# Second score products of two 64-wide attentions: 128 rows in place of 64, and one low-key tile per head in the neighbourhood attention

## The chip, the core and the metric

The kernel runs on one core of a Trainium2 chip. The core has TensorE (PE), VectorE (DVE), ScalarE (ACT), GpSimd (POOL) and SyncE (SP), which here issues every DMA of the stages in question. The metric is the device time of one execution in microseconds. Three timed runs of the kernel before took 1984.27, 1992.58 and 1996.03 us; the median is 1992.58 us.

## The reference, cut to what matters

A two-layer backbone over 1024 latent tokens and 256 context tokens, feature width 1024. Layer 0 joins a differential attention of 4 heads with a latent attention of 8 heads; layer 1 joins an mLSTM with a neighbourhood attention of 8 heads. Two of these attentions have query and key vectors of 64 values: the differential one (two score maps per head) and the neighbourhood one. Cut to the scores:

```python
DA_HEADS, DA_QK = 4, 64
NA_HEADS, NA_DH = 8, 64
...
q1, q2, k1, k2 = (to_heads(t, DA_HEADS) for t in (q1, q2, k1, k2))
...
s_nb = jnp.einsum('bqhd,brqjhd->bhqrj', q_r, k_nb).astype(F32) * NA_SCALE + bias
s_cx = jnp.einsum('bqhd,bthd->bhqt', q_r, k_ctx).astype(F32) * NA_SCALE
p = jax.nn.softmax(jnp.concatenate([s_nb.reshape(b, h, GRID_W, n_nb), s_cx], axis=-1), axis=-1)
```

Each differential head takes softmax(q1 k1) minus a factor times softmax(q2 k2). In the neighbourhood attention each query sees a window of 8 x 16 grid cells and all 256 context tokens.

## The kernel before

Products of high accuracy are made of two parts: a value is split into a high part, which PE takes as it is, and a low part, the rest. A score is q_high k_high + q_low k_high + q_high k_low; the product of the two low parts is left out.

For 64-wide heads the kernel uses the 128 rows of PE like this. The query tile holds the high part of q in one half of its 128 partitions and the low part in the other. The high key tile kh holds the same 64 rows twice, in both halves. One product of 128 rows then gives (q_high + q_low) k_high. A second product adds q_high k_low; it uses 64 rows, namely the half in which q_high stands, and the low key tile kl.

**Attention stage of layer 0** (class `Differential`, and `Latent` for the other heads). For each differential head and each of its two score maps b, `load_scores` (L536) fills one tile `o` of 128 x 4 x 1280: slot 0 is q, slot 1 kh, slot 2 kl. It issues five DMAs of 320 KB: q and kh for each half (L543, L544), and kl for partitions 0 to 63 (L545). `load_values` (L547) loads the values and the gate. There is one tile `o` per map, so the next head's load of a map waits until the last score product of the head before has read it. For each row tile of 128 queries, `cut` (L562) issues the score products in pieces of at most 512 keys: L568 with kh (128 rows), L569 with kl (64 rows). Latent row tiles have products of 96 rows (L720 to L722). Scores go to one of two PSUM tiles `s`; DVE finds the row maximum (L1151), ACT the exponentials (L1158), DVE combines the two maps (L588); PE transposes the result into one of two banks `tp` (L1175), ACT and DVE copy it out (L518), and PE forms the value products (L599, L745).

**Neighbourhood stage of layer 1** (class `Neighbours`). Each of the 8 heads h has 8 steps (hf, g). `load` (L2094) gets q, kh, kl, the gate and, for even heads, the values in 16 pieces. Two units may be loaded at a time. kl is one shared tile for all heads: an even head uses partitions 0 to 63, an odd head 64 to 127, and each fills only its own half (L2111, one DMA of 320 KB). For odd heads the halves of q are swapped, so that q_high is in the half of kl. A step's `scores` (L2137) issues four products: L2143 (kh, 384 neighbourhood keys, 128 rows), L2144 (kl, 64 rows), L2145 (kh, 256 context keys, 128 rows), L2146 (kl, 64 rows). DVE adds the bias and finds the maximum (L2151), ACT takes exponentials (L2157), POOL scales (L2164). After two steps PE transposes the pair (L2191), copies follow (L518), then the value products (L2205). Between the steps stand filler products: gate products (L2030 to L2032), and at the end the first half of the output projection (L2289 to L2291).

In both stages the order of the instructions comes from a planner, `Plan` (L428): a task names its engine, a cost, the tasks it follows and the buffers it takes and gives back. The planner issues the task that can start earliest by its own account. Each engine then runs its instructions in that order, SP its DMA issues too.

Of the kernel before, what the change touches and what calls it, by code (L numbers as in the profile page):

```python
# [137 lines left out]
def hybrid_kernel(ctx, tc, t, out, dbg=None):  # L138
# [111 lines left out]
    def ada_first(f, w, pool, psum):  # L250
        """The layer's shift and scale of one block of 128 features."""
        ps = psum.tile([P, 512], F32, name="mm")
        for k in range(KT):
            g = 32 * (k % 4)
            T.matmul(ps[g:g + 32, :256], sil[:, k, :], w[:, k, :], start=k < 4, stop=k >= 4)
        part = pool.tile([P, 256], F32, name="part0", bufs=2)
        V.tensor_copy(out=part, in_=ps[:, :256])
        ps = psum.tile([P, 512], F32, name="mm")
        for i in range(2):
            T.matmul(ps[:, 2 * i:2 * i + 2], part[:, i * P:(i + 1) * P], cst[:, C_SEL:C_SEL + 2], start=True, stop=True)  # L260
            b = V0["ab0"] + 8 * i + f
            V.tensor_scalar(out=mods[0][:, 8 * i + f, :], in0=ps[:, 2 * i:2 * i + 2], scalar1=vt[0][:, b:b + 1],
                            scalar2=float(i), op0=ALU.add, op1=ALU.add)
# [130 lines left out]
    # ---------------------------------------------------------------- layer 0: projections  # L394
# [27 lines left out]
    class Join:  # L422
        """A buffer that several tasks give back together."""
# [4 lines left out]
    class Plan:  # L428
        """Orders the instructions of a pipelined phase: every task names its engine, about how long it holds it, what
        it follows and which buffers it takes or gives back; the earliest possible task is issued next. Kinds of  # L430
        tasks can lean: count as that much later (or earlier) than they could start."""
# [79 lines left out]
    def moves(plan, bank, dst, m, last, cut=3):  # L511
        """Copies m blocks of 128 columns out of a bank, in parts that the engines take as they come."""
        parts = [(0, m)] if m < cut else [(0, m // 2), (m // 2, m)]
        join = Join("tp", len(parts))
        left = list(parts)

        def move(eng, c0, c1):
            copy_by(eng)(out=dst()[:, c0:c1, :], in_=bank()[:, c0 * P:c1 * P].rearrange("p (c q) -> p c q", q=P))  # L518
            left.pop()
            if not left:  # L520
                given("tp", bank())
        return [plan.add("AV", (on_scalar((c1 - c0) * P, False), on_vector((c1 - c0) * P)), partial(move, c0=c0, c1=c1),
                         [last], [], [join], rank=R2) for c0, c1 in parts]
# [7 lines left out]
    class Differential(Unit):  # L531
# [4 lines left out]
        def load_scores(self, pool, b):  # L536
            h = self.h
            r = slice(64 * (h % 2), 64 * (h % 2) + 64)
            o = pool.tile([P, 4, NT], FR, name=f"o{b}")
            self.q[b], self.kh[b], self.kl[b] = o[:, 0, :], o[:, 1, :], o[0:64, 2, :]  # L540
            for i in range(2):
                hb = slice(64 * i, 64 * i + 64)
                dma(out=self.q[b][hb, :].bitcast(F32), in_=s_qk[b][i][h // 2, r, :])  # L543
                dma(out=self.kh[b][hb, :].bitcast(F32), in_=s_qk[2 + b][0][h // 2, r, :])  # L544
            dma(out=self.kl[b].bitcast(F32), in_=s_qk[2 + b][1][h // 2, r, :])  # L545
# [11 lines left out]
        def plan(self, tt):  # L557
# [4 lines left out]
            def cut(b, n0, nn):  # L562
                def emit(_):
                    if n0 == 0:
                        x["s", b] = taken("s")
                    s, ql = x["s", b], self.q[b][:, tt * P:(tt + 1) * P]
                    ks = slice(k0 * P + n0, k0 * P + n0 + nn)
                    T.matmul(s[:, n0:n0 + nn], ql, self.kh[b][:, ks], start=True, stop=False)  # L568
                    T.matmul(s[:, n0:n0 + nn], ql[0:64], self.kl[b][:, ks], start=False, stop=True)  # L569
                return emit  # L570
# [61 lines left out]
        def finish(self, t0, n, last):  # L632
            """A group of row tiles: the root mean square of every row, the gain and the gate."""
# [189 lines left out]
    with space(name="pa", bufs=1) as pa, space(name="psa", bufs=1, space=PSUM) as psa0, ExitStack() as wa_stack:  # L823
# [8 lines left out]
        def load_x(g, q):  # L832
            """A quarter of the features of a group of row tiles."""
            t0, n = TG[g]
            src = t["x"][0] if t0 < LT else t["ctx"][0]
            r0 = t0 % LT * P
            x = xp.tile([P, 4, 256], F32, name="xt", bufs=8)[:, 0:n]
            dma(out=x, in_=src[r0:r0 + n * P, q * 256:(q + 1) * 256].rearrange("(a p) n -> p a n", p=P))
            xs[g, q] = x
# [8 lines left out]
        def first_products(g, k):  # L848
            """Adds feature block k to the first weights' products of a group of row tiles, two tiles to a bank."""
# [288 lines left out]
    # ---------------------------------------------------------------- layer 0: attention  # L1138
# [154 lines left out]
    # ---------------------------------------------------------------- output projection and layer norm  # L1293
# [103 lines left out]
    # ---------------------------------------------------------------- layer 1: mLSTM  # L1397
# [337 lines left out]
    # ---------------------------------------------------------------- layer 1: projections and mLSTM  # L1735
# [107 lines left out]
    with space(name="hidc", bufs=1, side="right") as hq, space(name="zt", bufs=2, side="right") as zt, \  # L1843
# [84 lines left out]
        def chunk():  # L1928
            """The weights loaded ahead, and the load of those after the next."""
# [52 lines left out]
    # ---------------------------------------------------------------- layer 1: neighbourhood attention  # L1982
# [3 lines left out]
    with space(name="nf", bufs=1, side="right") as nf, space(name="psf", bufs=1, space=PSUM) as psf:  # L1986
# [101 lines left out]
        class Neighbours:  # L2088
# [5 lines left out]
            def load(self):  # L2094
# [3 lines left out]
                if "kl" not in sh:  # L2098
                    sh["kl"] = nf.tile([P, NT], FR, name="kl")
# [4 lines left out]
                self.kl, self.gate, self.bias = sh["kl"], sh["gate"], sh["bias"]  # L2104
# [6 lines left out]
                dma(out=self.kl[r, :].bitcast(F32), in_=s_kn[1][p, r, :])  # L2111
# [8 lines left out]
                self.v, self.x = sh["v"]  # L2120

# [6 lines left out]
            def plan(self, plan, hf, g):  # L2128
# [8 lines left out]
                def scores(_):  # L2137
# [6 lines left out]
                    T.matmul(s[:, 128:512], q[ws], kl[ws], start=False, stop=True)  # L2144
                    T.matmul(s[:, 512:768], q, self.kh[:, NLAT:NT], start=True, stop=False)  # L2145
                    T.matmul(s[:, 512:768], q[ws], self.kl[ws, NLAT:NT], start=False, stop=True)  # L2146
# [19 lines left out]
                if hf == 0 and g == 0:  # L2166
                    self.ready = plan.add("D", 14.0 if self.h % 2 == 0 else 5.0, lambda _: self.load(),
                                          stores if self.h >= 4 else [], ["unit"])
                if g == 0:
# [3 lines left out]
                self.first = last = plan.add("P", 0.54, scores, [self.ready], ["s"])  # L2173
# [53 lines left out]
        plan = Plan("neighbours", s=2, tp=2, mm=2, np=4, npt=2, eo=2, e=2, hv=2, raw=1, wr=1, unit=2, bt0=1, bt1=1, slot=0, y=2, nyy=1)  # L2227
# [8 lines left out]
        def settle_half(_):  # L2236
            """The second half of the layer's hidden rows is used up: half of the output projection's weights goes there."""
# [35 lines left out]
        def first_half(tt, opened, ready):  # L2273
            """A row tile's residual with the half of the output projection's sum that the mLSTM's features give."""
# [84 lines left out]
```

## Time and profile before

| what | value |
|---|---|
| timed runs | 1984.27, 1992.58, 1996.03 us |
| span of the profiled execution | 1998.1 us |
| span against the median | 5.5 us more |
| PE busy | 1923.2 us (96%) |
| DVE busy | 1078.6 us (54%) |
| ACT busy | 785.6 us (39%) |
| mean granted clock of PE | 0.975 |
| differential score products | from 462.4 to 975.1 us of the span |
| neighbourhood score products | from 1636.6 to 1887.7 us of the span |

The profile comes from one execution. Its own time is known as the span alone, from the first to the last instruction; it stands 2.1 us above the slowest timed run. In the rows of a timeline the columns are the start, the time, the engine, the line, the operation, what it writes and reads, rows * columns of PE in use, and the tile that it reads; behind them, in brackets, idle time before it and what ended that. Matmuls are pipelined and their ends are modelled, so two starts in a row tell more than one duration. In the rows of a window stand the length of the stretch, the busy time of PE, PE's weight load, DVE, ACT and POOL, then PE's granted clock (1.00 is full), the busy share of the DMA engines and what they moved in GB/s.

### The profile page before, as it was taken

How to read it: one execution, taken by the hardware profiler on the slowest of the kernel's cores; microseconds unless marked ns; L12 is line 12 of the kernel's file. 1: busy time of each engine (PE TensorE's matmuls, PEld its weight loads, DVE VectorE, ACT ScalarE, POOL GpSimd, SP SyncE). 2: the span in 40 equal slices, each digit the busy share in tenths (PEclk: the TensorE clock that was granted, in tenths of full speed). 3: DMA queues.
4: the chain of work that ended last, by engine and by line, in shares of the span. 5: the costliest groups of instructions: out<-in, count | busy, mean ns of one | idle time of the engine just before them, and what ended most of it. 6: DMA issues, size and time to landing. Idle time of an engine off the chain costs nothing.

```text
span 1998.1 us, 33063 instructions
## 1 busy us (share of the span) xinstructions
PE 1923.2 (96%) x12493; PEld 1590.8 (80%) x12493; DVE 1078.6 (54%) x2267; ACT 785.6 (39%) x1627; POOL 530.3 (27%) x651
## 2 busy tenths in 40 slices
PE   7999999999999999999999989999998999999998
PEld 5888998886777777778787879888898877777676
DVE  3653124313666666656665854765766125566756
ACT  2311024423556555555662312334543233344521
POOL 1433233100132222323363432220111002223434
PEclk9999999997899999999999999999999999999999
DMA  9757425675130550540566442226452365466552
GB/s 282 230 198 227 139 68 155 196 197 132 30 88 6 125 130 9 127 122 12 139 191 229 138 143 74 82 76 184 146 142 66 116 209 137 130 172 172 157 164 84
DMA packets 241475, 270.93 MB, mean 136 GB/s; under 512 B 24914, under 2 KB 203038, under 8 KB 241318
## 3 DMA queue, kind: packets, MB, share of 16 engines
q1 hardware_dynamic: 241318, 268.83, 46.9%
q8 instruction: 99, 1.62, 0.4%
q14 instruction: 58, 0.48, 0.1%
HBM read 187.90 MB, written 87.16 MB: 138 GB/s over the span
## 4 chain that ended last, share of the span: by engine, by line
PE 69%; DMA 8%; DVE 3%; SPq 1%; issue 1%; ACT 1%; POOL 0%; DVEq 0%; POOLq 0%; ACTq 0%
PE mm L390 7%; PE mm L392 7%; PE mm L391 7%; PE tp L1175 5%; PE s L569 4%; PE tp L745 3%; PE tp L599 3%; PE s L568 3%; PE mm L1778 3%; PE mm L1779 3%; PE mm L1780 3%; PE mm L2030 2%; PE tp L2205 2%; PE tp L2191 2%; DMA o<-s_qk 2%; PE s L720 2%
## 5 line engine op out<-in xcount | busy, mean ns | idle before, releaser
L1151 DVE TENSOR_REDUCE nm<-s 128x1 f32<-128x1280 f32 (+1 forms) x160 | 203.9, 1276 | 139.8 <-PE s L569 117.4
L1158 ACT ACTIVATE p<-s,nm 128x1280 f32<-128x1280 f32 (+1 forms) x160 | 185.4, 1159 | 68.1 <-DVE nm L1151 42.0
L737 POOL TENSOR_SCALAR p<-p,zs 128x512 f32<-128x512 f32 (+1 forms) x208 | 128.3, 633 | 309.9 <-DVE zs L733 282.6
L518 ACT COPY pt<-tp 128x256 f32<-128x256 f32 x346 | 119.3, 375 | 153.8 <-PE tp L1175 145.8
L1175 PE MATMUL tp<-cst,p 128*128 128x128 f32 x1008 | 162.1, 285 | 4.7 <-DVE pt L518 2.2
L347 POOL TENSOR_TENSOR wlo<-raw,whi 128x1024 fp32r<-128x1024 f32 (+2 forms) x41 | 98.9, 2413 | 214.8 <-ACT whi L339 210.3
L1175 PEld LDWEIGHTS tp<-cst,p 128*128 128x128 f32 x1008 | 117.1, 144 | 42.4 <-issue 19.6
L390 PE MATMUL mm<-whi,hhi 128*128 128x256 f32 (+1 forms) x496 | 147.6, 298 | 0.3 <-DVE z L975 0.3
L392 PE MATMUL mm<-whi,hlo 128*128 128x256 f32 (+1 forms) x496 | 146.6, 296 | 0.2 <-DVE hlo L290 0.2
L391 PE MATMUL mm<-wlo,hhi 128*128 128x256 f32 (+1 forms) x496 | 146.4, 295 | 0.0
L339 ACT CAST whi<-raw 128x1024 fp32r<-128x1024 f32 (+2 forms) x54 | 55.9, 1035 | 172.0 <-DMA raw<-in_ev_w_in_dram 71.6
L2164 POOL TENSOR_SCALAR np<-np,nrz 128x640 f32<-128x640 f32 x64 | 53.5, 838 | 241.3 <-DVE nrz L2161 236.8
L518 DVE COPY pt<-tp 128x256 f32<-128x256 f32 x158 | 64.3, 422 | 76.9 <-ACT pt L518 61.5
L569 PE MATMUL s<-o 64*128 64x512 f32 (+1 forms) x208 | 99.6, 479 | 3.3 <-DMA o<-s_qk 3.3
L568 PE MATMUL s<-o 128*128 128x512 f32 (+1 forms) x208 | 96.7, 465 | 5.7 <-DMA o<-s_qk 4.0
L390 PEld LDWEIGHTS mm<-whi,hhi 128*128 128x128 f32 x496 | 94.6, 191 | 2.6 <-issue 1.7
L392 PEld LDWEIGHTS mm<-whi,hlo 128*128 128x128 f32 x496 | 94.5, 191 | 0.5 <-DVE hlo L290 0.4
L391 PEld LDWEIGHTS mm<-wlo,hhi 128*128 128x128 f32 x496 | 94.6, 191 | 0.2
L720 PE MATMUL s<-o 96*128 96x512 f32 (+1 forms) x208 | 89.0, 428 | 0.6 <-ACT p L1158 0.6
L599 PE MATMUL tp<-v,pt 128*128 128x128 f32 x672 | 85.7, 283 | 0.0
L745 PE MATMUL tp<-pt,v 128*64 128x128 f32 x1344 | 84.3, 280 | 0.4 <-ACT pt L518 0.2
L599 PEld LDWEIGHTS tp<-v,pt 128*128 128x128 f32 x672 | 81.2, 198 | 3.1 <-DVE pt L518 0.8
(451 smaller groups left out, 5052.8 us busy)
## 6 DMA issues: line engine op xcount, KB each, us to landing
adaw<-in_ada_w_dram SPq DMA_DIRECT2D x16, 1024.0 KB
raw<-in_od_w_in_dram SPq DMA_DIRECT2D x32, 512.0 KB
o<-s_qk SPq DMA_DIRECT2D x40, 320.0 KB
raw<-in_ev_w_in_dram SPq DMA_DIRECT2D x18, 512.0 KB
bt<-s_bt SPq DMA_DIRECT2D x16, 576.0 KB
adaw<-in_ada_w_dram SPq DMA_DIRECT2D x16, 512.0 KB
o<-s_mq SPq DMA_DIRECT2D x16, 480.0 KB
s_gate<-e SPq DMA_DIRECT2D x24, 256.0 KB
```

The lines of the kernel that those rows point to most:

```text
L390: T.matmul(ps, ahi(k), bhi(k), start=k == k0, stop=False)
L391: T.matmul(ps, ahi(k), blo(k), start=False, stop=False)
L392: T.matmul(ps, alo(k), bhi(k), start=False, stop=k == nk - 1)
L518: copy_by(eng)(out=dst()[:, c0:c1, :], in_=bank()[:, c0 * P:c1 * P].rearrange("p (c q) -> p c q", q=P))
L568: T.matmul(s[:, n0:n0 + nn], ql, self.kh[b][:, ks], start=True, stop=False)
L569: T.matmul(s[:, n0:n0 + nn], ql[0:64], self.kl[b][:, ks], start=False, stop=True)
L599: T.matmul(o[:, :P], x["pt"][:, c, :], self.v[:, k0 + c, :], start=c == 0, stop=c == nch - 1)
L720: T.matmul(s[:, n0:n0 + nn], self.qh[a][:, qsl], self.kh[a][:, ks], start=True, stop=False)
L745: T.matmul(o[64 * b:64 * b + 64, :P], self.v[:, k0 + c, b * 64:(b + 1) * 64], pair[b]["pt"][:, c, :], start=c == 0, stop=c == nch - 1)
L1151: V.tensor_reduce(out=nm, in_=s[:, :w], axis=AX.X, op=ALU.max, negate=True)
L1158: S.activation(out=p[:, :w], in_=s[:, :w], func=AF.Exp, bias=nm, accum_out=z)
L1175: T.transpose(ps[:, c * P:(c + 1) * P], p()[:, (c0 + c) * P:(c0 + c + 1) * P], ident)
```

## The change

Both second products use all 128 rows. kl is now held in both halves, so the product is (q_high + q_low) k_low; the term q_low k_low, which was left out, is in it.

In the attention stage slot 2 of the tile `o` has all 128 partitions, and L545 stands inside the loop over the halves: six DMAs of 320 KB for each map, not five. Tile sizes and the planner's costs stay the same there.

In the neighbourhood stage the shared kl goes. `load_low` fills one kl tile (one buffer) for each head with two DMAs of 320 KB. It is a task of its own that follows the head's `load` and takes the buffer `kl`; the last step of a head gives it back, and the first products of a head wait for it. The cost of a step's scores in the plan goes from 0.54 to 0.58. The score products stand in L2147 to L2150 now, the transpositions in L2197, the value products in L2211, the fillers of the output projection in L2295 to L2297.

```diff
-            self.q[b], self.kh[b], self.kl[b] = o[:, 0, :], o[:, 1, :], o[0:64, 2, :]
+            self.q[b], self.kh[b], self.kl[b] = o[:, 0, :], o[:, 1, :], o[:, 2, :]
             for i in range(2):
                 hb = slice(64 * i, 64 * i + 64)
                 dma(out=self.q[b][hb, :].bitcast(F32), in_=s_qk[b][i][h // 2, r, :])
                 dma(out=self.kh[b][hb, :].bitcast(F32), in_=s_qk[2 + b][0][h // 2, r, :])
-            dma(out=self.kl[b].bitcast(F32), in_=s_qk[2 + b][1][h // 2, r, :])
+                dma(out=self.kl[b][hb, :].bitcast(F32), in_=s_qk[2 + b][1][h // 2, r, :])
...
-                    T.matmul(s[:, n0:n0 + nn], ql[0:64], self.kl[b][:, ks], start=False, stop=True)
+                    T.matmul(s[:, n0:n0 + nn], ql, self.kl[b][:, ks], start=False, stop=True)
...
-                dma(out=self.kl[r, :].bitcast(F32), in_=s_kn[1][p, r, :])
...
+            def load_low(self):
+                p, a = self.h // 2, self.h % 2
+                self.kl = nf.tile([P, NT], FR, name="kl", bufs=1)
+                for i in range(2):
+                    dma(out=self.kl[64 * i:64 * i + 64, :].bitcast(F32), in_=s_kn[1][p, 64 * a:64 * a + 64, :])
...
-                    T.matmul(s[:, 128:512], q[ws], kl[ws], start=False, stop=True)
+                    T.matmul(s[:, 128:512], q, kl, start=False, stop=True)
...
-                    T.matmul(s[:, 512:768], q[ws], self.kl[ws, NLAT:NT], start=False, stop=True)
+                    T.matmul(s[:, 512:768], q, self.kl[:, NLAT:NT], start=False, stop=True)
...
+                    self.ready_low = plan.add("D", 4.0, lambda _: self.load_low(), [self.ready], ["kl"], rank=0)
...
-                self.first = last = plan.add("P", 0.54, scores, [self.ready], ["s"])
+                self.first = last = plan.add("P", 0.58, scores, [self.ready, self.ready_low], ["s"],
+                                             ["kl"] if hf and g == 3 else [])
...
-        plan = Plan("neighbours", s=2, tp=2, mm=2, np=4, npt=2, eo=2, e=2, hv=2, raw=1, wr=1, unit=2, bt0=1, bt1=1, slot=0, y=2, nyy=1)
+        plan = Plan("neighbours", s=2, tp=2, mm=2, np=4, npt=2, eo=2, e=2, hv=2, raw=1, wr=1, unit=2, kl=1, bt0=1, bt1=1, slot=0, y=2, nyy=1)
```

In the attention stage the order on PE, DVE, ACT and POOL stays as it was. In the neighbourhood stage the planner gives another order. Two places of it follow; names carry the buffers' numbers.

PE at the change from head 6 to head 7, before: the first two steps of head 7 (L2143 to L2146) with what stands ahead of and between them; `tp` are transposition banks, `np` probabilities, `npt` their transposes, `vn` and `vx` values.

```order
L2191 MATMUL tp_15064<-cst,np_15067 128x128 x4
L2205 MATMUL tp_15063<-npt_15072,vn 64x128 x6
L2205 MATMUL tp_15063<-npt_15072,vx 64x128 x4
L2191 MATMUL tp_15064<-cst,np_15067 128x128
L2191 MATMUL tp_15064<-cst,np_15068 128x128 x3
L2143 MATMUL s_15061<-kh,q 128x384
L2144 MATMUL s_15061<-kl,q 128x384
L2145 MATMUL s_15061<-kh,q 128x256
L2146 MATMUL s_15061<-kl,q 128x256
L2191 MATMUL tp_15063<-cst,np_15068 128x128 x2
L2143 MATMUL s_15062<-kh,q 128x384
```

The same place on PE in the changed program (L2147 to L2150 are the scores, L2197 the transpositions, L2211 the value products):

```order
L2197 MATMUL tp_15072<-cst,np_15075 128x128
L2197 MATMUL tp_15072<-cst,np_15076 128x128 x3
L2197 MATMUL tp_15071<-cst,np_15076 128x128 x2
L2211 MATMUL tp_15072<-npt_15079,vn 64x128 x6
L2211 MATMUL tp_15072<-npt_15079,vx 64x128 x4
L2147 MATMUL s_15069<-kh,q 128x384
L2148 MATMUL s_15069<-kl,q 128x384
L2149 MATMUL s_15069<-kh,q 128x256
L2150 MATMUL s_15069<-kl,q 128x256
L2147 MATMUL s_15070<-kh,q 128x384
```

The first scores of head 7 moved behind all transpositions and the value products of head 6's last pair.

SP at the same head change, before: the loads of a head (q, kh, kl and the gate `ngt`), a bias table `bt` and stores of results.

```order
L2109 DMA q<-s_qn_11132 64x1024
L2110 DMA kh<-s_kn_11133 64x1280
L2109 DMA q<-s_qn_11131 64x1024
L2110 DMA kh<-s_kn_11133 64x1280
L2111 DMA kl<-s_kn_11134 64x1280
L2112 DMA ngt<-s_gate 64x1024
L2123 DMA bt_15095<-s_bt 128x3x384
L2219 DMA s_y<-nyy 64x512
```

And in the changed program:

```order
L2108 DMA q<-s_qn_11140 64x1024
L2109 DMA kh<-s_kn_11141 64x1280
L2108 DMA q<-s_qn_11139 64x1024
L2109 DMA kh<-s_kn_11141 64x1280
L2110 DMA ngt<-s_gate 64x1024
L2127 DMA bt_15102<-s_bt 128x3x384
L2124 DMA kl<-s_kn_11142 64x1280 x2
L2225 DMA s_y<-nyy 64x512
```

The low keys moved from the middle of the head's load to a place of their own behind the bias table, and there are two transfers where there was one.

More of the change, by code (lines that the diff above doesn't have):

```diff
@@ L2097, in load @@
                 sh = self.shared
-                if "kl" not in sh:
-                    sh["kl"] = nf.tile([P, NT], FR, name="kl")
+                if "gate" not in sh:
                     sh["gate"] = nf.tile([P, NLAT], F32, name="ngt")
@@ L2103, in load @@
                         G.memset(y[:, :, 384:640], 0.0)
-                self.kl, self.gate, self.bias = sh["kl"], sh["gate"], sh["bias"]
+                self.gate, self.bias = sh["gate"], sh["bias"]
                 self.q = nf.tile([P, NLAT], FR, name="q", bufs=2)
```

## The prediction

> **What bounds the kernel now.** I began with the head of the page and its chain that ended last, to see which engine carries the end, and then cut out the two stages that the change touches.
>
> ```profile
> span 1998.1 us, 33063 instructions
> PE 69%; DMA 8%; DVE 3%; SPq 1%; issue 1%; ACT 1%; POOL 0%; DVEq 0%; POOLq 0%; ACTq 0%
> ...
> 460.00:980.00 520.00, 507.46 (x3448) 387.40 (x3447) 324.79 (x588) 294.69 (x696) 128.39 (x219) 0.95 0.33 78
> 1636.00:1890.00 254.00, 252.93 (x1550) 179.45 (x1549) 147.25 (x345) 110.00 (x226) 73.95 (x76) 1.00 0.60 155
> ```
>
> PE is 69% of the chain. The two window rows are the attention stage (differential and latent heads mixed, 520 us) and the neighbourhood stage (254 us). In both PE is busy for over 97% of the stage, while DVE stands at 62% and 58% and ACT at 57% and 43%. The view of PE's waits in these stages shows almost none:
>
> ```profile
> PE s L568 <- DMA o<-s_qk: 4.0, 2, 2.3
> ...
> PE tp L1175 <- DVE pt L518: 1.5, 6, 0.3
> ```
>
> So time taken out of PE shortens both stages until another engine or a load is late. But a busy PE need not be a PE that streams. The timeline of PE, read from start to start, shows where it does not:
>
> ```profile
> 603.81 0.47 PE L720 MATMUL s<-o 96*128 96x512 f32 x1
> 604.12 0.39 PE L721 MATMUL s<-o 96*128 96x512 f32 x1
> 604.35 0.39 PE L722 MATMUL s<-o 96*128 96x512 f32 x1
> ...
> 606.07 0.28 PE L721 MATMUL s<-o 96*128 96x256 f32 x1
> 606.18 0.28 PE L722 MATMUL s<-o 96*128 96x256 f32 x1
> ...
> 607.10 0.48 PE L568 MATMUL s<-o 128*128 128x512 f32 x1
> 607.51 0.49 PE L569 MATMUL s<-o 64*128 64x512 f32 x1
> 607.93 0.50 PE L568 MATMUL s<-o 128*128 128x512 f32 x1
> 608.36 0.50 PE L569 MATMUL s<-o 64*128 64x512 f32 x1
> 608.79 0.44 PE L1175 MATMUL tp<-cst,p 128*128 128x128 f32 x2
> 608.98 0.36 PE L568 MATMUL s<-o 128*128 128x256 f32 x1
> 609.28 0.38 PE L569 MATMUL s<-o 64*128 64x256 f32 x1
> 609.59 2.50 PE L599 MATMUL tp<-v,pt 128*128 128x128 f32 x20
> ```
>
> The latent heads' 96-row products (L720 to L722) follow one another after 0.23 us at 512 columns and 0.11 to 0.12 at 256. The differential heads alternate between 128 rows (L568) and 64 rows (L569), and there each start stands 0.42 to 0.43 us after the last at 512 columns, 0.30 to 0.31 at 256. The columns are the same, so some 0.2 us at each change of row count is no streaming.
>
> **The change, attention stage.** L569 becomes a 128-row product like its neighbours. The code gives 208 of them in 4 heads: 128 of 512 columns, 80 of 256. By the rows above 512 columns go from 0.42 to 0.23 and 256 from 0.31 to 0.12, 0.19 each: 208 x 0.19 = 40 us. L568 gains in two sizes. Where it follows an L569 directly (83 of 208 in the program's order) it goes from 0.43 to 0.23, 83 x 0.2 = 17 us. Elsewhere it follows a transposition or a value product and keeps that start: L720 after transpositions takes 0.31, L568 takes 0.41, so 125 x 0.09 = 11 us. **Gross 68 us.** What comes first after an L569 may also start sooner; I leave that out.
>
> What the 0.2 us hid can now be late. First the loads. Each score tile set of a head is now six 320 KB transfers, not five, and L569 waits for the last:
>
> ```profile
> 704.78 0.47 PE L568 MATMUL s<-o 128*128 128x512 f32 x1 [2.28 <-DMA o<-s_qk]
> 706.16 0.50 PE L569 MATMUL s<-o 64*128 64x512 f32 x1 [0.91 <-DMA o<-s_qk]
> ...
> 545.51 6.77 DMA o<-s_qk
> 552.30 9.87 DMA o<-s_qk
> ```
>
> The chain of waits gives 16.64 us for ten such transfers, 1.66 each, and at a head change PE already waits for them (2.28 and 0.91). Two more make 3.3 us, at three head changes 10 us; with nothing hidden and PE early by another 1 to 2 us it would be 15, and if the second set hides its part, 5. The first head's transfers are issued 28 us before use and cost nothing. Second the copies out of the transposition banks:
>
> ```profile
> L518 ACT COPY pt<-tp 128x256 f32<-128x256 f32 x346 | 119.3, 375 | 153.8 <-PE tp L1175 145.8
> ```
>
> There are two such banks. 87 groups of transpositions stand directly behind an L569 and will come 0.2 to 0.4 us sooner, about one copy of 0.375. If all had been just in time, 87 x 0.4 = 35 us would come back as waits; with slack, none. The 1.5 us of waits now lie near the lower end, but DVE goes from 62% to 69% (324.79 of 473), so I take 11. **Net for the stage: 68 - 10 - 11 = 47 us.**
>
> **The change, neighbourhood stage.** 64 steps (8 heads of 8), four products each, now in the timeline of a filled stretch:
>
> ```profile
> 1704.99 0.45 PE L2143 MATMUL s<-kh,q 128*128 128x384 f32 x1
> 1705.36 0.44 PE L2144 MATMUL s<-kl,q 64*128 64x384 f32 x1
> 1705.73 0.38 PE L2145 MATMUL s<-kh,q 128*128 128x256 f32 x1
> 1706.05 0.38 PE L2146 MATMUL s<-kl,q 64*128 64x256 f32 x1
> 1706.36 0.50 PE L2030 MATMUL mm<-h,whi 128*128 128x512 f32 x1
> 1706.69 0.40 PE L2031 MATMUL mm<-h,whi 128*128 128x512 f32 x1
> 1706.93 0.39 PE L2032 MATMUL mm<-h,wlo 128*128 128x512 f32 x1
> ```
>
> From L2143 to L2031 it is 1.70 us. Without changes of row count: 0.37 - 0.1 for the first, which still follows another form; 0.17 for 384 columns, between the 0.12 and 0.23 above; twice 0.12; and 0.24 for L2030: 0.92. **Gross 64 x 0.77 = 49 us**, as not every step is followed by L2030.
>
> Now the new wait. The low-key tile is single and filled afresh for each head. Its two transfers are issued only when the previous head's last score product has read the old one, and on the same SP queue the next bias table, stores of results and the next head's loads stand behind them. The first score product of the new head waits for both halves. No row shows this transfer alone; the nearest is a bias table of 576 KB on a quiet queue:
>
> ```profile
> 1737.37 0.37 SPq L2123 DMA_DIRECT2D bt<-s_bt  x1
> ...
> 1740.00:1741.00 1.00, 1.00 (x7) 0.56 (x3) 0.57 (x2) 0.00 (x0) 1.00 (x1) 1.00 0.88 314
> 1741.00:1742.00 1.00, 1.00 (x7) 0.77 (x7) 0.38 (x1) 0.00 (x0) 1.00 (x1) 1.00 0.00 0
> ```
>
> Issued at 1737.37, its bytes are through by 1741: 3.6 us. 640 KB in two issues makes 4.0 + 0.6. The new order puts nine filler products or none, a pair's transpositions (or two pairs') and their value products there: about 4.6 us of PE. So the wait is 0 to 0.6 us alone, and some 3 us more where another 512 KB transfer runs just ahead. At seven head changes: 0 to 25 us, I take 5. The stores and tables behind it on SP are wanted several steps later.
>
> The new order also lets the pipeline run empty where fillers lack (rows in the section on the change): a head's first scores no longer stand ahead of the last head's transpositions. What PE then waits for is one pass through three engines:
>
> ```profile
> L2157 ACT ACTIVATE np<-np,nnm 128x640 f32<-128x640 f32 x64 | 53.1, 829 | 59.4 <-DVE nnm L2151 51.6 <-DVE nrz L2161 7.6
> L2151 DVE CUSTOM_DVE_ANT_0 np<-s,bt 128x640 f32<-128x640 f32 x64 | 52.2, 822 | 46.7 <-PE s L2146 35.2 <-POOL np L2164 5.3 <-issue 3.7
> L2164 POOL TENSOR_SCALAR np<-np,nrz 128x640 f32<-128x640 f32 x62 | 51.9, 839 | 239.2 <-DVE nrz L2161 234.7 <-PE mm L2032 4.3
> ```
>
> 0.82 + 0.83 + 0.84 is 2.5 us, 3 with the small steps between. Two head changes have no filler (into heads 4 and 7), with such a wait before and after: 4 x 3 = 12 at most, none at least; with the last two heads, which have little filler throughout, I take 11. **Net: 49 - 5 - 11 = 33 us.**
>
> **Sum.** 47 + 33 = 80 us against the profiled 1998.1, which makes 1918. That execution is 5.5 us above the median of the timed runs, 1992.58; carried over, 1992.6 - 80 = **1912 us**.
>
> **Rivals.** *A, half is taken back.* Copies hold all 87 groups (35 us), loads cost 15, head changes of the neighbourhood stage 25 + 12: 117 - 87 = 30 us at worst, 1963; half way between that and the forecast, 55 us, about 1938. For it: DVE and ACT serve both ends of every chain. Against it: their shares leave 30% free and PE hardly waits today.
>
> *B, the row count is not the cause.* If each product had to wait for its own weight load, 0.19 us, and then stream 0.23, that would be the 0.42 seen, and the change would give nothing: 1992 us.
>
> ```profile
> 1706.70 0.19 PEld L2032 LDWEIGHTS mm<-h,wlo 128*128 128x128 f32 x1
> ```
>
> Against it: this load runs while L2031 does (1706.69 to 1707.09), and L2032 starts 0.24 after it. The Trainium skill, page "TensorE: Matmul & The Clock Gate", Part 3, says that a weight load overlaps products in flight only where the row group differs; by it 128 rows behind 128 rows would not overlap, the step would stay at 0.42 and the time at 1992. The row above contradicts it.
>
> *C, slower: the clock.* A short wait already halves PE's clock:
>
> ```profile
> 467.81 0.79 PE L568 MATMUL s<-o 128*128 128x512 f32 x1 [0.69 <-ACT p L1158]
> ...
> 467.80:488.30 20.50, 20.50 (x48) 11.71 (x49) 10.19 (x14) 8.57 (x15) 0.00 (x0) 0.50 0.94 218
> ```
>
> After 0.69 us of waiting the granted clock is 0.50 for 20.5 us, some 10 us lost. If a PE that now waits for DVE and ACT sets this off again and again in the attention stage, more than eight such stretches there eat the 80 us, and twelve make 2030. Against it: the stage has 0.95 on the mean, and PE will stream a larger share of its time than now. The Trainium skill, the same page, Part 1, has the clock fall only after an idle window of about 3.4 us; by it C would need far longer waits, but the 0.69 us speak against that reading.
>
> **How the numbers follow.** Forecast 0.72 (1880 to 1930), A 0.18, B 0.05, C 0.05. The lower end is 1992.6 - 117 = 1876, nothing taken back; the upper end takes in most of A. Range 1875 to 1952. A difference under 0.5% (10 us) could not be told from none. Faster 0.90 (forecast and A), same 0.05 (B), slower 0.05 (C).
>
> **What will show it.** Right: L569 and the low-key products L2148 and L2150 as 128*128, 0.23 or less after their predecessors; the attention window near 473 us and the neighbourhood window near 221; L569's waits for s_qk near 3 us more per head change; a new wait for kl at most heads, under 1 us. Wrong: steps of 0.42 in spite of 128 rows (B); long waits of L1175 for the copies (A); a granted clock well under 0.95 in the attention window (C).

## The result and the profile after

The changed kernel takes **1921.64 us** (median of four runs, 1917.45 to 1925.9), beside 1990.7 us for the kernel before, measured with it (four runs, 1984.27 to 1996.03). The ratio is 0.9653, 95% interval 0.9628 to 0.9678: 69 us faster. The forecast was 1912 us in a range of 1875 to 1952. The profiled execution spans 1923.8 us, 74.3 less than that of before. It is the slowest of the four runs, and the profile of before is at the slow end too, so a stage's length in one profile is good to a few us only.

The head of the page and its chain that ended last, changed kernel:

```profile
span 1923.8 us, 33069 instructions
...
PE 62%; DMA 9%; DVE 5%; issue 2%; ACT 2%; SPq 2%; POOL 0%; DVEq 0%; POOLq 0%; ACTq 0%
```

PE falls from 69% to 62% of the chain, DMA and DVE rise from 8% and 3% to 9% and 5%. So PE still carries the end, but other engines now have a larger part in it. The windows of the two stages, cut to their new ends (columns: window, its length, busy time of PE, of PE's weight load PEld, of DVE, ACT and POOL, granted clock, DMA share, GB/s):

```profile
460.00:928.00 468.00, 434.33 (x3430) 377.09 (x3428) 323.09 (x588) 292.37 (x695) 128.88 (x218) 0.96 0.39 90
1584.00:1814.00 230.00, 212.10 (x1539) 176.57 (x1538) 148.93 (x345) 106.48 (x215) 69.63 (x75) 0.97 0.69 181
```

Before, PE was busy for 98% of the attention window and over 99% of the neighbourhood one; now it is 93% and 92%. DVE's work is the same (323 and 149 us) in less time. And in the neighbourhood stage the granted clock, 1.00 before, is 0.97. From the first L568 to the last L569 it is 463.1 us (before 513.0), from the first to the last neighbourhood score product 228.0 (before 251.2).

PE's timeline in the attention stage, start and length in us:

```profile
599.22 0.48 PE L568 MATMUL s<-o 128*128 128x512 f32 x1
599.54 0.39 PE L569 MATMUL s<-o 128*128 128x512 f32 x1
599.77 0.39 PE L568 MATMUL s<-o 128*128 128x512 f32 x1
...
601.23 0.28 PE L569 MATMUL s<-o 128*128 128x256 f32 x1
601.34 0.39 PE L720 MATMUL s<-o 96*128 96x512 f32 x1
601.57 0.39 PE L721 MATMUL s<-o 96*128 96x512 f32 x1
```

From the L569 at 599.54 to the next start it is 0.23 us (before 0.42; the L568 ahead of it, which follows other work, still takes 0.32), and behind the L569 of 256 columns at 601.23 it is 0.11 (before 0.31). The neighbourhood stage reads the same way:

```profile
1649.67 0.42 PE L2147 MATMUL s<-kh,q 128*128 128x384 f32 x1
1649.93 0.34 PE L2148 MATMUL s<-kl,q 128*128 128x384 f32 x1
1650.10 0.28 PE L2149 MATMUL s<-kh,q 128*128 128x256 f32 x1
1650.22 0.28 PE L2150 MATMUL s<-kl,q 128*128 128x256 f32 x1
1650.34 0.39 PE L2030 MATMUL mm<-h,whi 128*128 128x512 f32 x1
1650.57 0.40 PE L2031 MATMUL mm<-h,whi 128*128 128x512 f32 x1
```

From the first score product to L2031 it is 0.90 us; before it was 1.70, and the forecast said 0.92. So the steps shrank as forecast. PE's waits show what was given back, first in the attention stage, then in the neighbourhood stage (total, times, longest, in us):

```profile
PE s L721 <- DMA o<-s_kr: 9.2, 3, 5.6
PE s L568 <- DMA o<-s_qk: 8.6, 5, 3.5
PE s L568 <- ACT p L1158: 7.8, 10, 1.9
PE s L569 <- DMA o<-s_qk: 6.0, 6, 1.2
...
PE tp L1175 <- DVE pt L518: 0.2, 1, 0.2
...
PE tp L2197 <- DVE nyy L2219: 5.8, 3, 4.5
PE tp L2197 <- POOL np L2168: 4.8, 4, 1.7
PE s L2147 <- DVE nnm L2155: 4.3, 1, 4.3
PE tp L2211 <- DVE npt L518: 2.9, 4, 1.3
PE s L2148 <- DMA kl<-s_kn: 2.8, 1, 2.8
```

In the attention stage the loads (`o`) and ACT's exponentials (`p`), which hold the score buffers, are late; the copies out of the transposition banks (`pt`) are not. In the neighbourhood stage nearly every engine that serves PE is late somewhere.

### The profile page after: what moved, and what is told of

It is laid out like the page before. It is cut to its first block, busy times and chain, and to the rows that moved or that the text cites. A ratio compares the mean times of both kernels' runs of the same rounds, so it can differ in the third digit from the quotient of the medians.

```text
span 1923.8 us, 33069 instructions
## 1 busy us (share of the span) xinstructions
PE 1811.8 (94%) x12493; PEld 1579.9 (82%) x12493; DVE 1083.7 (56%) x2273; ACT 782.2 (41%) x1622; POOL 527.2 (27%) x650
## 4 chain that ended last, share of the span: by engine, by line
PE 62%; DMA 9%; DVE 5%; issue 2%; ACT 2%; SPq 2%; POOL 0%; DVEq 0%; POOLq 0%; ACTq 0%
PE mm L390 7%; PE mm L392 7%; PE mm L391 7%; PE tp L1175 4%; PE tp L745 4%; DMA o<-s_qk 3%; PE tp L599 3%; PE mm L1778 3%; PE mm L1779 3%; PE mm L1780 3%; PE s L569 2%; DMA o<-s_kr 2%; PE s L568 2%; PE s L720 2%; PE tp L2211 2%
## 5 line engine op out<-in xcount | busy, mean ns | idle before, releaser
L1175 PE MATMUL tp<-cst,p 128*128 128x128 f32 x1008 | 157.0, 279 | 3.8 <-DVE zs L733 1.4
L568 PE MATMUL s<-o 128*128 128x512 f32 (+1 forms) x208 | 86.7, 419 | 16.4 <-DMA o<-s_qk 8.6
L720 PE MATMUL s<-o 96*128 96x512 f32 (+1 forms) x208 | 87.8, 422 | 1.4 <-ACT p L1158 1.4
L721 PE MATMUL s<-o 96*128 96x512 f32 (+1 forms) x208 | 74.8, 360 | 9.4 <-DMA o<-s_kr 9.4
```

What stands on the lines that cost most here:

```text
L720: T.matmul(s[:, n0:n0 + nn], self.qh[a][:, qsl], self.kh[a][:, ks], start=True, stop=False)
L1175: T.transpose(ps[:, c * P:(c + 1) * P], p()[:, (c0 + c) * P:(c0 + c + 1) * P], ident)
```

## The experiments

In what follows "from the first score to the end" is the time from the first neighbourhood score product to the end of the span: 361.3 us before, 339.4 in the changed kernel. Every kernel was measured with the kernel before, whose median was 1990.7 to 1995.9 us from case to case; by the ratios, differences from the changed kernel come out up to 6 us larger than by the times below.

### One part at a time

The first kernel is before with L536 to L569 of the change alone, the second with the neighbourhood part alone:

```diff
+                dma(out=self.kl[b][hb, :].bitcast(F32), in_=s_qk[2 + b][1][h // 2, r, :])
...
-                    T.matmul(s[:, n0:n0 + nn], ql[0:64], self.kl[b][:, ks], start=False, stop=True)
+                    T.matmul(s[:, n0:n0 + nn], ql, self.kl[b][:, ks], start=False, stop=True)
```

> Only the differential heads' part of the change is made; the neighbourhood stage is as before. If the two parts are independent, the attention stage loses the 50 us that it lost in the changed kernel and the neighbourhood stage keeps its 251 us from first to last score product: about 1941 us. Rival: part of what the attention stage gains depends on nothing here but shows up again as waits in the stages behind it; then it gives less than 40 us, above 1951.

> Only the neighbourhood part is made; the attention stage is as before (513 us from the first L568 to the last L569). If the parts are independent: 22 us less than before, about 1968 us, with the same new waits as in the changed kernel (first bias table at the stage's start 4 to 5 us, copies out of the transposition banks, POOL's product). Rival: the waits at the stage's start come from the earlier end of the attention stage; then the bias table is not waited for here and the gain is about 28 us.

Attention alone: 1936.42 us against 1992.26, ratio 0.9714 (0.9694 to 0.9734), **56 us**. Neighbours alone: 1977.71 us, ratio 0.9917 (0.9892 to 0.9943), **15 us** (11 to 22). Together 70, and the whole change gave 69: within the intervals the parts are independent, and the first expectation's rival falls. The second expectation, 1968 us, was missed by 10: the neighbourhood part gives 15 us, not 22. The attention stage of the first kernel is 455.8 us long, 57 less than before and 7 less than in the changed kernel's profile, although both run the same instructions there. The waits of the first kernel in that stage show where those 7 us lie:

```profile
PE s L568 <- DMA o<-s_qk: 11.6, 5, 4.4
...
PE s L569 <- DMA o<-s_qk: 5.0, 6, 1.0
PE s L721 <- DMA o<-s_kr: 4.3, 3, 1.7
```

It waits 4.3 us for the latent heads' loads (`s_kr`) where the profile of the changed kernel has 9.2, and no more than 1.7 at once. In all PE is idle for 3 us less there and busy for 4 us less, with the clock at half for 30.7 us and not 41.0. The long wait varies between executions, and the changed kernel's profile caught a long one: four kernels here with the same instructions in this stage take 454.2 to 456.7 us for it. The neighbours-alone kernel has the same waits in its stage as the changed one, that for the first bias table among them:

```profile
PE s L2147 <- DVE nnm L2155: 3.9, 1, 3.9
```

So that wait does not come from an earlier end of the attention stage: the rival falls. From the first score to the end it takes 337.9 us, 20 less than the attention-alone kernel (358.2, its neighbourhood stage being that of before). The profiled execution is the fastest of the four timed runs (1970.91, median 1977.71), so 15 is the better figure for the whole.

### Is it the change of row count, or the 64 rows?

In the kernel before, three 64-row products make each differential score tile (the added one reads the low queries from a fourth slot of tile `o`):

```diff
-                    T.matmul(s[:, n0:n0 + nn], ql, self.kh[b][:, ks], start=True, stop=False)
+                    T.matmul(s[:, n0:n0 + nn], ql[0:64], self.kh[b][0:64, ks], start=True, stop=False)
+                    T.matmul(s[:, n0:n0 + nn], self.ql[b][:, tt * P:(tt + 1) * P], self.kh[b][0:64, ks], start=False, stop=False)
                     T.matmul(s[:, n0:n0 + nn], ql[0:64], self.kl[b][:, ks], start=False, stop=True)
```

> The kernel before, in which each differential score tile is made by three 64-row products (high by high, low by high, high by low keys) instead of one of 128 and one of 64 rows; the neighbourhood stage is as before. If the 0.2 us goes to the change of row count, the second and third of the three follow 0.23 us after their predecessors at 512 columns and 0.12 at 256, and only the first, behind 128-row work, and the first 128-row product after the three pay it: the attention stage stays within 15 us of before although it has half as many products again. If a 64-row product as such costs 0.42 us, all three have that step and the stage grows by 208 steps of 0.42 or 0.31, some 78 us.

One timed run took 2002.11 us (before 1995.86), and the attention stage 526.5 us: 208 more products for 13 us. PE's timeline there:

```profile
606.65 0.50 PE L570 MATMUL s<-o 64*128 64x512 f32 x1
606.99 0.39 PE L571 MATMUL s<-o 64*128 64x512 f32 x1
607.22 0.39 PE L572 MATMUL s<-o 64*128 64x512 f32 x1
...
607.91 0.39 PE L572 MATMUL s<-o 64*128 64x512 f32 x1
608.23 0.44 PE L1178 MATMUL tp<-cst,p 128*128 128x128 f32 x2
```

Between 64-row products the step is 0.23 us, as between 128-row ones; 0.32 lie between the last and the transpositions. (The first takes 0.34, but behind transpositions a 128-row product takes 0.32 too.) So 64 rows lengthen no step; a change does, about 0.1 us on each side of it. The traces of before and of the changed kernel say the same: L568 of 512 columns takes 0.425 us between two 64-row products (median of 39), 0.330 between a 96-row and a 64-row one (8 cases), and in the changed kernel, with no 64-row product beside it, 0.235. In the alternation of before every product stood between two changes and paid 0.2. Rival B is refuted from this side too.

### What the low-key loads cost in the attention stage

The second product reads the high keys again and no low keys are loaded, so the scores are not those of the reference; only the time counts:

```diff
-                dma(out=self.kl[b][hb, :].bitcast(F32), in_=s_qk[2 + b][1][h // 2, r, :])
...
-                    T.matmul(s[:, n0:n0 + nn], ql, self.kl[b][:, ks], start=False, stop=True)
+                    T.matmul(s[:, n0:n0 + nn], ql, self.kh[b][:, ks], start=False, stop=True)
```

> The changed kernel without the differential heads' low-key loads; their second product reads the high keys, so that term is left out there. If the three 320 KB transfers more per head change (and the two that were there already) cost PE's waits for s_qk, s_qk falls from 14.6 us to 5 or less and the kernel gets 8 to 12 us faster than the changed one. If the waits are set by when the buffers come free and not by the bytes, less than 4 us.

1898.4 us, ratio 0.9519 (0.9496 to 0.9543): 23 us below the changed kernel, twice what was expected, though PE's waits for `s_qk` fell less than expected, to 7.5 us. The stage's windows, the attention-alone kernel first, then this one, show why:

```profile
461.20:916.90 455.70, 425.30 (x3392) 369.33 (x3390) 319.97 (x575) 289.94 (x686) 128.81 (x218) 0.97 0.39 90
```

```profile
459.90:894.20 434.30, 415.03 (x3392) 361.83 (x3390) 319.49 (x575) 289.84 (x686) 128.30 (x218) 0.99 0.36 86
```

The stage is 21.4 us shorter. 11 of them are time in which PE is not busy (455.7 - 425.3 = 30.4, now 434.3 - 415.0 = 19.3). The other 10 are busy time, for the same number of matmuls: the clock is granted at 0.99 and not 0.97, at half for 6.8 us and not 30.7. So a late load can be paid twice, once as a wait and once as half clock behind it; which waits do that is told in the last section.

### The first head's bias table

The changed kernel, with head 0's table planned ahead of its low keys:

```diff
-                    self.ready_low = plan.add("D", 4.0, lambda _: self.load_low(), [self.ready], ["kl"], rank=0)
                 if g == 0:
                     self.ready_bias = plan.add("D", 1.7, lambda _: self.load_bias(hf), [self.shared.get(hf, self.ready)], [f"bt{hf}"],
                                                rank=0)
                     self.shared[hf] = self.ready_bias
+                if hf == 0 and g == 0:
+                    self.ready_low = plan.add("D", 4.0, lambda _: self.load_low(), [self.ready], ["kl"], rank=0)
```

> The changed kernel with the first head's bias table loaded ahead of its low-key tile on the SP queue. If that queue's order makes the first scores wait, the wait of 4.3 us behind nnm at 1587.8 and the half clock after it go: 4 to 6 us less than the changed kernel, 1916 or so. Rival: the table is late anyway because the stores of s_qn stand ahead of it on the queue; then no difference (within 1 us).

1922.28 us, ratio 0.9647 (0.9627 to 0.9668): no difference. SP's issues before the stage, changed kernel and then this one:

```profile
1575.05 1.74 SPq L2124 DMA_DIRECT2D kl<-s_kn  x2
...
1585.61 0.32 SPq L1819 DMA_DIRECT2D s_qn<-hv  x1
1585.98 0.43 SPq L2127 DMA_DIRECT2D bt<-s_bt  x1
```

```profile
1568.16 1.00 SPq L2127 DMA_DIRECT2D bt<-s_bt  x1
...
1578.72 0.32 SPq L1819 DMA_DIRECT2D s_qn<-hv  x1
1579.09 1.09 SPq L2124 DMA_DIRECT2D kl<-s_kn  x2
```

Stores of `s_qn`, whose data come at their own pace, stand between the two loads on the one queue. Whichever load is second waits for the last of them. With the table first, the low keys are late:

```profile
PE s L2148 <- DMA kl<-s_kn: 12.2, 4, 6.9
```

So the first theory falls: the wait of 4.3 us is gone and one of 6.9 us takes its place. The rival named the right stores but not the right load.

### The single low-key tile: its transfers and its place in the order

Two kernels leave the low keys of the neighbourhood stage out and read the high keys twice. The first keeps the planner's task for them:

```diff
-                self.kl = nf.tile([P, NT], FR, name="kl", bufs=1)
-                for i in range(2):
-                    dma(out=self.kl[64 * i:64 * i + 64, :].bitcast(F32), in_=s_kn[1][p, 64 * a:64 * a + 64, :])
+                self.kl = self.kh
```

The second takes the task out as well:

```diff
-                    self.ready_low = plan.add("D", 4.0, lambda _: self.load_low(), [self.ready], ["kl"], rank=0)
+                    self.ready_low = self.ready
...
-                                             ["kl"] if hf and g == 3 else [])
+                                             [])
```

> The changed kernel, in which the neighbourhood stage loads no low keys and its second product reads the high keys instead, so the low-key term is left out there; the planned order is kept. If the single low-key tile's own transfers cost time (its wait, and the stores and bias tables behind its 640 KB on the SP queue), the stage gets shorter by 5 us or more. If what was taken back comes from the order of the steps and from the three-engine passes, it stays within 3 us of the changed kernel: the one wait for kl was 2.8 us, so about 2 to 3 us less.

> As e3_low_reads_kh (no low keys in the neighbourhood stage, the low-key term left out there), but the planner has no load of a low-key tile to place either, so that the order of the steps is free of it. If the planned wait for the single tile makes the pipeline run empty at the head changes (the waits for POOL, for the copies and for the gated product), these waits go and it is 8 us or more faster than e3_low_reads_kh, 1906 or less. If the order costs nothing and only the shorter products let the engines' chain through, within 4 us of e3_low_reads_kh (1910 to 1918).

Without the transfers: 1914.14 us, ratio 0.9600 (0.9578 to 0.9622). From the first score to the end it takes 334.9 us, **4.5 less** than the changed kernel: the wait for kl and a little more, and between the two expectations. (The timed runs differ by 7.5; the rest lies in the attention stage, where the instructions are the same.) Without the task as well: 1900.65 us, ratio 0.9520 (0.9486 to 0.9553), and 321.8 us from the first score to the end, **13 less again**. With the task, the planner may place a head's first scores only 7.1 us behind the last head's last score: the task's 4.0, 2.5 that it adds to every load, and two hops of 0.3. In the trace of the first of these kernels the gaps from a head's last score product to the next head's first are 6.2 to 9.4 us, 53 in all as in the changed kernel; without the task they make 36, in the kernel before 35. That order is what costs, since nothing else differs between the two kernels. The two longest rows of PE's waits from the first score on, without the task:

```profile
PE tp L2196 <- DVE nyy L2218: 3.5, 4, 1.7
PE mm L2294 <- DVE r L2300: 3.1, 1, 3.1
```

The 4.8 us behind POOL's product and the 4.3 us behind the first table are gone. The rest stays, 11.3 us in all its rows, where the attention-alone kernel has 2.6: a faster PE finds DVE and ACT late even with this order.

### Zeros for the second half

The rows of the second half of a low-key tile need not be loaded. POOL sets them to zero once, and the products keep their 128 rows (in the neighbourhood stage the high queries then always lie in the lower half, so that zeros and keys keep their places):

```diff
+                self.shared[b] = pool.tile([P, 4, NT], FR, name=f"o{b}")
+                G.memset(self.shared[b][64:128, 2, :].bitcast(F32), 0.0)
...
-                dma(out=self.kl[b][hb, :].bitcast(F32), in_=s_qk[2 + b][1][h // 2, r, :])
+            dma(out=self.kl[b][0:64, :].bitcast(F32), in_=s_qk[2 + b][1][h // 2, r, :])
...
-                    self.ready_low = plan.add("D", 4.0, lambda _: self.load_low(), [self.ready], ["kl"], rank=0)
+                    self.ready_low = plan.add("D", 2.0, lambda _: self.load_low(), [self.ready], ["kl"], rank=0)
```

> The changed kernel with the second half of each low-key tile set to zero once, by POOL, and never loaded again: the products keep their 128 rows, the low by low term is zero as it was before the change, and each head loads one low-key transfer and not two, in both stages. If the doubled transfers are what costs, attention's waits for s_qk return to the 7 us of before and the neighbourhood stage comes near that of e3_low_reads_kh: 8 to 14 us faster than the changed kernel. If the bytes do not matter, within 3 us of it.

**1894.02 us**, ratio 0.9491 (0.9467 to 0.9515), and in a second measurement 1894.71, ratio 0.9515 (0.9486 to 0.9544). That is 27 us faster than the changed kernel, and the fastest version here that loads its low keys. In its profile the attention stage is 444.9 us long, 11 less than with attention alone (439.9 in the second, 16 less), and 328.4 us lie between the first score and the end, 11 less than in the changed kernel. That is more than the 8 to 14 expected, though attention's waits for `s_qk` did not return to 7 us (10.7, and 9.3 in the second). Clock comes with the waits again (0.98 in its attention window), and the planner's cost for the load is 2.0 here and not 4.0, so the order in the neighbourhood stage changed as well:

```profile
460.00:910.00 450.00, 427.38 (x3435) 371.01 (x3433) 322.28 (x584) 291.79 (x693) 129.05 (x218) 0.98 0.38 90
```

The planner's cost of the low-key load was then lowered, beside a second measurement:

```diff
-                    self.ready_low = plan.add("D", 2.0, lambda _: self.load_low(), [self.ready], ["kl"], rank=0)
+                    self.ready_low = plan.add("D", 0.6, lambda _: self.load_low(), [self.ready], ["kl"], rank=0)
```

> As e10_zero_half, but the planner takes the load of the low-key tile for 0.6 us and not 2.0, so that it places a head's first scores sooner behind the last head's. The tile is still single. If the order is what costs (pipeline empty at the head changes), the neighbourhood stage comes near that of e8_no_low_task, 211 us from first to last score product, and the kernel is 5 us or more faster than e10_zero_half. Rival: the real wait for the tile (2 us or more at each of seven head changes, PE idle in it) takes the place of the planned one; then PE shows waits for kl of 10 us or more and it is equal or slower than e10_zero_half.

> As e11_low_cost_06 with 1.2 us: half way. By the first theory 2 to 4 us faster than e10_zero_half; by the rival within 2 us of it or slower, with waits for kl of 5 us or more.

> The same kernel as e10_zero_half, beside the two others on one chip: 1894 us, ratio to before 0.949. A difference of over 3 us from its first measurement would make the comparison of the planner's costs unsafe.

With 0.6 it took 1899.02 us (ratio 0.9542, 0.9506 to 0.9579), with 1.2 it took 1895.04 (0.9514, 0.9483 to 0.9544), beside 1894.71 with 2.0. No lower cost is faster. With 2.0 PE shows no wait for kl; with 1.2 it waits 6.2 us at four head changes, and with 0.6 at six of the seven:

```profile
PE s L2156 <- DMA kl<-s_kn: 6.6, 6, 2.4
```

The rival holds in kind, though with 0.6 not in size (6.6 us, not 10): the planned gap and the real wait look like two forms of one cost, that of a single tile. A second tile was not tried, so that it would end this cost is not shown.

## Why the prediction was right, and where it was off

- **PE bounds both stages, and the 0.2 us is the change of row count.** Right. The three products of 64 rows and the steps of 0.23 and 0.12 us after the change show it.
- **Attention, gross 68 us.** Right. L569's 208 steps lost 0.19 to 0.20 each, the 83 L568 behind an L569 0.19, the other 125 some 0.09: 68 us. What was left out, the step from the first transposition behind an L569 to the next instruction (median 0.165 us before, 0.109 now), adds 0.06 x 87 = 5. All these steps are at full clock.
- **Loads, minus 10.** Right for the waits: 16.6 us for `s_qk` with attention alone, 14.6 in the changed kernel, 7.3 before (other executions of the same new stage have 10.7 to 18.2). Zeros in place of the doubled transfers shorten the stage by 11 to 16. What the step did not have is the half clock behind the longer waits.
- **Copies, minus 11.** Wrong: the wait for them was 1.5 us before and is 0.2 now. In their place came the score buffers: L568 waits 7.8 us for ACT's exponentials (1.5 before). And the latent heads' loads, which the forecast did not look at, cost 1 to 7 us more than before, by the execution. PE's idle time in the stage rose from 12.5 to 33.6 us, which is just the 10 + 11 deducted; as some two thirds of the rise are waits for the score buffers and the latent heads' loads, which it did not count, that is luck.
- **Net 47 us in this stage.** The profile of the changed kernel gives 50; attention alone gave 56 in the timed runs. The term that is missing is the clock: the stage had 51.2 us at half clock before and has 30.7 with attention alone (41.0 in the changed kernel's profile). Each us at half clock costs about half a us, so 5 to 10 us came back that way. In the attention-alone profile the stage is 57 us shorter: some 65 from the steps and 10 from the clock, less 18 of new idle time.
- **Neighbourhood, gross 49 us.** Nearly right: L2148, L2149 and L2150 lost 0.19 to 0.20 us each in 64 steps, the first score product 0.09, and L2030 behind a low product 0.11 in some 40: 64 x 0.67 + 40 x 0.11 = 47.
- **The wait for kl, 5, and the pipeline that runs empty, 11.** Right in sum, not in place. The transfers cost 4.5 and the order 13, 17.5 against 16, in part by luck. The forecast did not have the planner's gap of 7.1 us at every head change. And the wait for kl came once (2.8 us), not at most heads, and the empty pipeline did not show as waits of 3 us at heads 4 and 7: it is spread over the waits for POOL, the copies and the gated product.
- **Net 33 us here.** Wrong: 15 in the timed runs, 19 to 20 by the profiles. The step that failed is "Net: 49 - 5 - 11 = 33": it charges what the new tile brings and nothing for an engine chain that serves a faster PE. The kernel without the tile shows it: of 47 us gross it keeps 36 (358.2 - 321.8), with 9 us more of waits for DVE and ACT than with attention alone. And it lacked the clock: this stage had 1.00 and has 0.97, four stretches of half clock behind waits, 13.7 us, which cost some 7. A last piece lies behind the last score product, where 111.4 us are left and 105.4 with attention alone. There PE stands behind DVE, which first scales the next weights:

```profile
1815.66 4.73 DVE L2263 TENSOR_TENSOR wlo<-wlo,gain 128x1024 f32<-128x1024 f32 x2
1820.31 3.37 DVE L2263 TENSOR_TENSOR raw<-raw,gain 128x1024 f32<-128x1024 f32 x1
1823.71 0.59 DVE L2219 TENSOR_TENSOR nyy<-tp,ngt 64x128 f32<-64x128 f32 x2
```

  The gated product `nyy`, which gives PE its bank back, comes behind 8 us of scaling, and PE waits 4.5 for it. But the profile of before has 110.1 us there, with the same scaling ahead of `nyy` and a wait of 3.0, though its instructions there are those of the attention-alone kernel. So it is not shown how much of this piece the change brings:

```profile
PE tp L2191 <- DVE nyy L2213: 3.0, 1, 3.0
```

- **The sum.** 1912 against 1921.6. The attention stage gave 3 to 9 us more than its term and the neighbourhood stage 13 to 18 less, so the two errors partly cancel, and that the sum is closer than its parts is luck. The 69 us measured lie about midway between the forecast's 80 and the 55 of rival A.
- **Rivals.** A named the copies, which hold nothing, but its other half, that the head changes take back their gain, is what the neighbourhood stage did. B is refuted by the steps after the change and by the three 64-row products. C did not come as such: attention's clock rose from 0.95 to 0.96 (0.97 with attention alone). Waits with half clock behind them do hold some 10 us there, as the kernel without low-key loads shows. But the prediction's reading of its row, that a wait of 0.69 us brought 20.5 us of half clock, does not carry over: in the stages whose second product has 128 rows, so little idle time was never followed by half clock (last section). In that row PE is busy for all 20.50 us and the clock stays at half, which those stages never show.

## What to carry to other kernels

Products whose row counts alternate pay at each change; give them one row count, with zeros if need be, and the second half then need not be loaded at all. When PE is busy all the time, price a shorter step with what its feeders can deliver: count the buffers and engines that were just in time, and where waits of 2 us or more come close together, take half clock behind them into account too. A single buffer that is filled afresh at each change of head cost a gap in the plan or a wait here, whichever of three numbers the planner was given.

## What the runs showed of the hardware

Between 96 and 128 rows nothing is lost, only between either and 64. Before, a 96-row product behind a 64-row one and the one after it:

```profile
595.73 0.38 PE L569 MATMUL s<-o 64*128 64x256 f32 x1
596.04 0.50 PE L720 MATMUL s<-o 96*128 96x512 f32 x1
596.38 0.39 PE L721 MATMUL s<-o 96*128 96x512 f32 x1
```

L720 stands 0.31 us after L569, and L721 0.34 after L720. In the changed kernel, where L569 has 128 rows (the rows from 601.23 to 601.57 above), L720 comes after 0.11, and L721 after 0.23.

In the profiles the clock changes in pieces of 3.4 us, and whether a piece is at half clock goes with PE's idle time in the piece before. The profiles here hold ten attention and ten neighbourhood stages whose second product has 128 rows. Of their 1711 pieces at full clock with less than 1.25 us idle, none was followed by half clock; of 47 with 2 us or more, all were; in between 20 of 75. So waits count when they come together. Behind the 4.3 us wait for the first bias table the window reads:

```profile
1591.70:1595.10 3.40, 2.94 (x9) 2.56 (x10) 2.11 (x8) 2.96 (x6) 0.46 (x1) 0.50 1.08 338
```

The wait of 5.6 us for the latent loads brought 10.2 us, three such pieces:

```profile
789.60:799.80 10.20, 6.06 (x20) 5.33 (x21) 1.89 (x4) 1.53 (x7) 1.33 (x4) 0.50 1.01 191
```

With 64-row products it is otherwise: half clock can come and stay without any wait. This is the neighbourhood stage of the attention-alone kernel, still with 64-row second products; in the first window PE runs score products of 128 and 64 rows by turns and is never idle, and the second is at half clock:

```profile
1690.60:1694.00 3.40, 3.40 (x12) 1.88 (x13) 2.33 (x8) 2.42 (x5) 1.30 (x2) 1.00 1.04 220
1694.00:1697.40 3.40, 3.40 (x13) 3.02 (x13) 2.55 (x4) 0.59 (x1) 1.08 (x2) 0.50 1.04 194
```

In three attention stages with 64-row products (before, neighbours alone, three of 64), 30 of 45 half-clock pieces with no idle time were followed by another; in the stages with 128-row second products none of 55 was. Since the kernel with three 64-row products shows it too, the changes of row count need not be the cause; which of the two it is, the runs do not separate.
